# A two-block network on one core: the expert table U split into float16 halves ahead of time and kept in DRAM

## The chip, the core and the metric

The kernel runs on one core of a Trainium2 chip. A core has a matrix engine (TensorE, PE in the profile), three engines that work on rows of 128 partitions (VectorE: DVE, ScalarE: ACT, GpSimd: POOL) and SyncE (SP), which here only issues transfers. Each engine carries out its own instructions strictly in order and waits on semaphores for the others. Sixteen DMA engines move data between DRAM and the on-chip memory; the transfers that one engine issues form a queue. The metric is the device time of one execution in microseconds (us).

## What is computed

Two transformer blocks follow each other for 512 tokens of width 1024, all in float32.

- The first block is a root-mean-square norm, three kinds of attention (a causal one with a forget gate, "fox"; a dilated one; one over compressed, selected and window keys, "NSA"), a gated sum of the three, and a gated feed-forward network with a short convolution.
- The second block is a norm, a mixer (short convolution and a gated linear recurrence) and PEER: a layer of 16384 experts, each a row of U and a row of V.

```python
q = (xt @ wq).reshape(t, PEER_HEADS, 2, HALF_Q)
scores = jnp.einsum('thpd,hpnd->thpn', q, keys)
s_top, i_top = lax.top_k(scores, PEER_TOPK)
cand = s_top[:, :, 0, :, None] + s_top[:, :, 1, None, :]
c_score, c_idx = lax.top_k(cand..., PEER_TOPK)
expert = i1 * N_KEYS + i2
gates = jax.nn.softmax(c_score, axis=-1)
u = jnp.take(u_tab, eb, axis=0)
a = jax.nn.gelu(jnp.einsum('td,thkd->thk', xb, u))
w = gb * a
vv = jnp.take(v_tab, eb, axis=0)
y = jnp.einsum('thk,thkd->td', w, vv)
```

## The kernel before, in words

**Products.** PE multiplies float16, so each float32 operand is split into a high half and a low half that together hold it, and each product is three matmuls (high by high, low by high, high by low). A weight block of 128 x 2048 float32 (1 MB) is loaded by SP into a tile `w` (`w_dma`, L136), ACT writes the high half `whi` (L144) and DVE the low half `wlo` (the helper `stt`, L72). The list `seq` fixes the order of all blocks that go this way; its last 64 blocks are the whole of U, transposed (`u_t`). The function `w_get` returns the next split block and keeps one further block split and one more loaded. Two `w` tiles are kept, and three pairs of halves.

**First block.** The norm and the first projections come first. The dilated attention follows; its three outputs are merged in `dil_merge` (L730 to L756: a maximum, three exponentials, a reciprocal and products, handed to and fro between DVE, POOL and ACT). Then come the fox attention, whose tables are built by PE from a triangular constant (`fox_tables`, L761; the constant `c_tri`, 128 x 1508 float32, loaded once at the start of the program, L462), and the NSA attention. Between the strips of the attention PE is given the remaining projections and gates as filling. The three outputs are multiplied by w_p and w_o, and the feed-forward (`conv_ffn`) follows: 22 blocks of w_up, each evacuated by ACT (`acc`), DVE (`acc`, `u`) and POOL (`ul`), then 12 blocks of w_down.

**Second block.** The mixer, the PEER queries, and the choice of the experts (called routing below): DVE finds the top 16 of many rows (`cand`, `cs`, `ci`), POOL and DVE turn the places into expert numbers (`eq` L1501, `sel` L1503), and PE transposes them (`pq`, L1526). 384 of the tokens are treated densely: all 16384 experts are computed as U times h, blocks of U being multiplied by 384 columns, 48 matmuls a block. A gate matrix G is built (`g`, `pg`), multiplied with the activations, and the result multiplied by V (64 more float32 blocks, split as `vh` and `vl`). The other 128 tokens gather their own rows of U and V: 128 gathers of each, issued by POOL (`row`, L1332). The first 12 blocks of U are multiplied beside the routing, 22 beside the building of G, and the last 30 in turn with blocks of V.

The order of the instructions on each engine is settled when the program is built, by a scheduler that simulates it; the code gives dependences and a rough order.

Of the kernel before, what the change touches and what calls it, by code (L numbers as in the profile page):

```python
# [9 lines left out]
F32 = mybir.dt.float32  # L10
# [8 lines left out]
S = 512  # L19
# [39 lines left out]
def tile_net(ctx: ExitStack, tc: tile.TileContext, xT, pp, cc, tn, btm, w_a, w_misc, cmp_w1, cmp_w2, cmp_pe,  # L59
# [68 lines left out]
    w32s, whs = {}, {}  # L128

    def w_dma():  # L130
        i = wst["dma"]
        if i >= len(seq):
            return
        t = wp.tile([128, 2048], F32, tag="w32", name="w32")
        n = seq[i].shape[1]
        nc.sync.dma_start(out=t[:, :n], in_=seq[i])  # L136
        w32s[i] = t[:, :n]
        wst["dma"] += 1
# [8 lines left out]
    def w_split():  # L147
        i = wst["split"]
        if i >= len(seq):
            return  # L150
        while wst["dma"] <= i:
            w_dma()
        t = w32s.pop(i)
        n = t.shape[1]
        pool = wst["more"] if wst["more"] is not None and i % 3 == 2 else wp
        hi = pool.tile([128, 2048], F16, tag="whi", name="whi")[:, :n]
        lo = pool.tile([128, 2048], F16, tag="wlo", name="wlo")[:, :n]
        split(t, hi, lo, wst["after"].pop(0) if wst["after"] else ())
        whs[i] = (hi, lo)
        wst["split"] += 1  # L160
# [10 lines left out]
    def mm3(ps, wh, wl, ah, al, idx, start=True, stop=True):  # L171

        n = len(idx)
        for j, i in enumerate(idx):
            mm(ps, wh(i), ah(i), start and j == 0, False)
            mm(ps, wh(i), al(i), False, False)
            mm(ps, wl(i), ah(i), False, stop and j == n - 1)

    def ps512(tag="mm", bufs=None):
# [173 lines left out]
    env = locals()  # L353
    attention(tc, nc, env)
    conv_ffn(tc, nc, env)
    mixer(tc, nc, env)
    peer(tc, nc, env)
# [91 lines left out]
def attention_core(tc, nc, env, ctx, yh, yl, gates, gate):  # L449
# [10 lines left out]
    while len(e.w32s) < 2:  # L460
        e.w_dma()
    e.load_consts(qp, nc.sync, "tri", "cmpm")  # L462

# [8 lines left out]
    nc.sync.dma_start(out=pe_t, in_=e.cmp_pe)  # L472


    F = {}
    scale_of = {t: 0.125 * DS if t in (0, 1, 4, 5, 6, 10, 11, 12) else DS for t in range(17)}

    def fm_tile(hi, lo, half, t, ps=None):
# [3 lines left out]
        if t in (13, 14):  # L482


            c = ap.tile([128, 2, 256], F32, tag="cf", name="cf", bufs=1)
            for g in range(2):
                rows = slice(64 * g, 64 * g + 64)
                for par in range(2):
                    SC.activation(out=c[64 * par:64 * par + 64, g, :], in_=ps[rows, par::2], func=ACTF.Identity, scale=DS,
                                  bias=bfm[rows, t:t + 1])  # L490
            for j in range(2):
                a = ap.tile([128, 2, 256], F32, tag="ca", name="ca", bufs=1)
# [3 lines left out]
                ch = qp.tile([128, 2, 256], F16, name=f"ch{t}{j}")  # L496
                cl = qp.tile([128, 2, 256], F16, name=f"cl{t}{j}")
# [338 lines left out]

    ptc = qp.tile([96, 4, 2, 128], F32, name="ptc")

    def cmp_probs(i):
# [25 lines left out]
        for g in range(2):  # L865
            PE.transpose(pt[0:96, g * 128:g * 128 + 128], st[:, 3 * g:3 * g + 3, :].rearrange("p h c -> p (h c)"), ident)
        V.tensor_copy(out=ptc[:, i], in_=pt[0:96, 0:256].rearrange("p (g c) -> p g c", g=2))

    def nsa_strips(r, sp):
# [4 lines left out]
        for i in range(4):  # L874
            n = 128 * (i + 1)
            for br in range(2):
# [3 lines left out]
                    gate=lambda p, i=i, br=br: gsig[:, i, 3 * (3 * p + r) + 1 + br:3 * (3 * p + r) + 2 + br],  # L880
                    extra=(lambda p, i=i: (F["vc"][32 * r:32 * r + 31, p, :], ptc[32 * r:32 * r + 31, i, p, :])) if br == 0 else None,
                    v=lambda b, p, br=br: T["vsw", b][:, br * 128 + p * 64:br * 128 + p * 64 + 64],
# [13 lines left out]
    for t in range(4):  # L896
        fm_tile(None, None, None, 4 + t, outs[t][2])
    e.x0s.close()
    dil = ExitStack()
    dp = dil.enter_context(tc.tile_pool(name="dp", bufs=1))  # L900
# [36 lines left out]
    dil.close()  # L937
    stk.append(ctx.enter_context(tc.tile_pool(name="stk", bufs=1)))
    with tc.tile_pool(name="fox", bufs=1) as sp:
        fox_tables(0, sp)  # L940
        run(fox_strips(0), n1 + (n2 - n1) // 2, NST - 1)
        fox_tables(1, sp)
        run(fox_strips(1), n2, NST - 1)
    with tc.tile_pool(name="nsa", bufs=2) as sp:
        rest = len(fill) - n2
# [875 lines left out]
```

## Time and profile before

| | us |
|---|---|
| median of 3 runs | 2386.96 |
| lowest and highest run | 2384.31, 2392.14 |
| the profiled execution | 2390.82 |
| span of its instructions | 2389.1 |

| engine | busy, share of the span |
|---|---|
| PE | 2278.6 us, 95% |
| DVE | 1682.6 us, 70% |
| ACT | 946.6 us, 40% |
| POOL | 783.1 us, 33% |

The mean granted clock of PE is 0.981 of its full 2.4 GHz. A busy PE is not PE at full rate: where the granted clock is 0.5, a matmul takes twice its time and counts as busy. So two figures are read together for each stretch: the time in which PE did nothing, and the clock.

### The profile page before, as it was taken

What the parts mean: (1) busy time and instruction counts of PE and PEld (TensorE: products, weight loads), DVE (VectorE), ACT (ScalarE), POOL (GpSimd) and SP (SyncE); (2) the same over time, 40 slices, a digit from 0 to 9 for tenths busy, and PEclk for the clock granted to TensorE, in tenths of its full rate; (3) what the DMA queues carried; (4) which work ended last, traced back from release to release, by engine and by line L of the source; (5) the groups of instructions that cost most, each with busy time, mean ns of one, the idle gap of its engine ahead of it and who ended that gap; (6) DMA issues with size and microseconds to landing.
All of it is one profiled execution on the core that took longest, in us unless ns stands there. A gap on an engine that the chain in (4) does not pass through costs nothing.

```text
span 2389.1 us, 35874 instructions
## 1 busy us (share of the span) xinstructions
PE 2278.6 (95%) x14415; PEld 1373.9 (58%) x14415; DVE 1682.6 (70%) x2996; ACT 946.6 (40%) x1256; POOL 783.1 (33%) x518
## 2 busy tenths in 40 slices
PE   7989999999999998999998789999999999989997
PEld 5646655456444466665745456665565555555665
DVE  5575556546444346554799989997898888899787
ACT  4454334334333226233424337775333332232332
POOL 1021000102222002220101541114667776778773
PEclk9998899999999999999999899999999999999998
DMA  5212321232222222211223548999999999899983
GB/s 195 89 36 89 119 69 54 88 106 89 106 106 96 98 90 94 88 54 71 108 87 132 185 151 315 341 328 358 350 345 348 358 342 342 320 370 389 379 304 124
DMA packets 143111, 460.64 MB, mean 193 GB/s; under 512 B 10864, under 2 KB 64496, under 8 KB 114656
## 3 DMA queue, kind: packets, MB, share of 16 engines
q1 hardware_dynamic: 92096, 280.02, 32.7%
q0 software_dynamic: 37600, 138.56, 15.6%
q10 hardware_dynamic: 13248, 39.76, 4.3%
q8 instruction: 113, 1.85, 0.3%
q14 instruction: 54, 0.44, 0.1%
HBM read 417.14 MB, written 40.63 MB: 192 GB/s over the span
## 4 chain that ended last, share of the span: by engine, by line
PE 59%; DVE 19%; issue 8%; DMA 6%; POOL 4%; ACT 3%; ACTq 0%; POOLq 0%; DVEq 0%; SPq 0%
PE mm L67 34%; PE y L67 5%; PE pa L67 5%; PE pb L67 5%; DVE wlo L72 3%; DMA row<-in_v_n,idx 3%; DVE row L1339 2%; DMA row<-in_u_n,idx 2%; PE o L67 2%; PE s L67 2%; PE p L67 2%; POOL row L1332 2%; POOL a L1622 1%; ACT whi L144 1%; PE t L643 1%
## 5 line engine op out<-in xcount | busy, mean ns | idle before, releaser
L67 PEld LDWEIGHTS <-whi 128*128 128x128 f16 x5384 | 530.1, 99 | 431.8 <-issue 42.8
L67 PE MATMUL mm<-hh,whi 128*128 128x384 f16 (+2 forms) x1640 | 566.7, 346 | 23.3 <-DVE x L72 11.9
L67 PE MATMUL mm<-hl,whi 128*128 128x384 f16 (+2 forms) x1640 | 567.3, 346 | 0.0
L67 PE MATMUL mm<-hh,wlo 128*128 128x384 f16 (+2 forms) x1640 | 566.8, 346 | 0.0
L72 DVE SCALAR_TENSOR_TENSOR wlo<-w,whi 128x2048 f16<-128x2048 f32 (+1 forms) x160 | 371.9, 2325 | 163.6 <-ACT whi L144 163.3
L144 ACT ACTIVATE whi<-w 128x2048 f16<-128x2048 f32 (+1 forms) x160 | 303.4, 1898 | 318.9 <-PE mm L67 219.6
L67 PEld LDWEIGHTS <-wlo 128*128 128x128 f16 x2692 | 266.8, 99 | 207.8 <-issue 9.6
L1332 POOL DMA_INDIRECT row<-in_u_n,idx x128 | 204.0, 1594 | 243.4 <-DVE atok L1339 225.7
L67 PEld LDWEIGHTS <-vh 128*128 128x128 f16 x2112 | 206.5, 98 | 131.2 <-issue 2.5
L144 ACT ACTIVATE vh<-w 128x2048 f16<-128x2048 f32 x64 | 119.0, 1903 | 345.0 <-PE mm L67 284.2
L1332 POOL DMA_INDIRECT row<-in_v_n,idx x128 | 211.0, 1649 | 108.9 <-DVE ytok L1356 81.0
L67 PE MATMUL y<-wl,vh 128*128 128x384 f16 (+2 forms) x660 | 212.8, 323 | 6.1 <-DVE wl L1624 5.9
L67 PE MATMUL y<-wh,vl 128*128 128x384 f16 (+2 forms) x660 | 212.8, 323 | 0.0
L67 PE MATMUL y<-wh,vh 128*128 128x384 f16 (+2 forms) x660 | 212.7, 323 | 0.0
L1356 DVE SCALAR_TENSOR_TENSOR ytok<-row,atok,ytok 128x1024 f32<-128x1024 f32 x127 | 184.6, 1453 | 26.6 <-DMA row<-in_v_n,idx 22.9
L1339 DVE CUSTOM_DVE_ANT_0 row<-row,htok 128x1024 f32<-128x1024 f32 x128 | 175.5, 1394 | 22.3 <-DMA row<-in_u_n,idx 22.1
L72 DVE SCALAR_TENSOR_TENSOR vl<-w,vh 128x2048 f16<-128x2048 f32 x64 | 153.5, 2412 | 25.5 <-ACT vh L144 25.4
L1622 POOL TENSOR_TENSOR a<-a,g 128x768 f32<-128x768 f32 x64 | 141.5, 2217 | 27.6 <-DMA g<-gd 18.0
L67 PEld LDWEIGHTS <-vl 128*128 128x128 f16 x1056 | 103.9, 98 | 71.4 <-issue 7.3
L67 PE MATMUL mm<-wh,vh 128*128 128x384 f16 (+2 forms) x396 | 126.6, 321 | 0.9 <-DVE x L72 0.9
L67 PE MATMUL mm<-wl,vh 128*128 128x384 f16 (+2 forms) x396 | 126.6, 321 | 0.0
L67 PE MATMUL mm<-wh,vl 128*128 128x384 f16 (+2 forms) x396 | 126.6, 321 | 0.0
(400 smaller groups left out, 3634.0 us busy)
## 6 DMA issues: line engine op xcount, KB each, us to landing
w<-in_u_t SPq DMA_DIRECT2D x64, 1024.0 KB
w<-in_v_t SPq DMA_DIRECT2D x64, 1024.0 KB
w<-in_w_a SPq DMA_DIRECT2D x24, 1024.0 KB
gd<-stage ACTq DMA_DIRECT2D x48, 512.0 KB
g<-gd SPq DMA_DIRECT2D x32, 768.0 KB
w<-in_w_up SPq DMA_DIRECT2D x22, 1024.0 KB
w<-in_w_mix SPq DMA_DIRECT2D x14, 1024.0 KB
ga<-a ACTq DMA_DIRECT2D x34, 384.0 KB
```

What stands on the lines that cost most here:

```text
L67: i = PE.matmul(out=out, lhsT=lhsT, rhs=rhs, start=start, stop=stop)
L72: (eng or V).scalar_tensor_tensor(out=out, in0=in0, scalar=scalar, in1=in1, op0=op0, op1=op1)
L144: SC.activation(out=hi, in_=t, func=ACTF.Copy, scale=WS)
L643: PE.transpose(ps[:, b * 128:b * 128 + 128], s.e[:, p, b * 128:b * 128 + 128], ident)
L1332: GP.indirect_dma_start(out=row, out_offset=None, in_=tab, in_offset=bass.IndirectOffsetOnAxis(ap=idx[:, s:s + 1], axis=0))
L1339: V.tensor_tensor_reduce(out=row, in0=row, in1=tok[kind[s // 32]], scale=1.0, scalar=0.0, op0=ALU.mult, op1=ALU.add, accum_out=atok[:, s:s ...
L1356: i = V.scalar_tensor_tensor(out=ytok[n], in0=row, scalar=w, in1=ytok[n], op0=ALU.mult, op1=ALU.add)
L1622: GP.tensor_tensor(out=by, in0=by, in1=g[:, :, i, :], op=ALU.mult)
```

## The change

Sixty-four blocks of U are split early. Each is cut in four quarters of 128 x 512. For a quarter POOL issues a load from `u_t` (256 KB, L143 of the changed file), ACT writes the high half and DVE the low half into a tile `ehl` (two of them exist; the loads have three), and POOL issues a store of both halves to a tensor `early` in DRAM (256 KB in 256 rows of 1 KB, L149). A step (`early_step`) stores the quarter split before, splits the next and issues the loads up to two quarters ahead; it is taken each time that PE has been given another 6100 columns of matmuls by `fm`, `tm` or `mm3`, from the dilated attention to the end of the feed-forward. What would be left then is done before the mixer.

In PEER a block of U then comes as two loads of 512 KB from `early`, straight into `whi` and `wlo`, with no work for ACT and DVE (L208, L209).

To make room, the constants `tri` to `cmpm` (the tile `c_tri`) and the tile `ptc` now lie in the pool `stk`, which is opened when the dilated attention's pool is closed, and are loaded there; some small tiles share buffers.

```diff
+NPRE = 64
+PACE = (6100, 6100)
...
+    dr0 = ctx.enter_context(tc.tile_pool(name="dr0", bufs=1, space=DRAM))
+    eps_ = ctx.enter_context(ExitStack())
+    ep = eps_.enter_context(tc.tile_pool(name="ep", bufs=3))
+    early = {len(seq) - 64 + k: dr0.tile([128, 2, 2048], F16, name=f"early{k}") for k in range(NPRE)}
+    es = {"load": 0, "split": 0, "store": 0, "cols": 0, "pace": 0, "t": {}, "h": {}}
+
+    def early_load():
+        q = es["load"]
+        if q < 4 * NPRE:
+            t = es["t"][q] = ep.tile([128, 512], F32, tag="e32", name="e32")
+            GP.dma_start(out=t, in_=u_t[q // 4][:, q % 4 * 512:q % 4 * 512 + 512])
+            es["load"] += 1
+
+    def early_store():
+        q = es["store"]
+        if q < es["split"]:
+            GP.dma_start(out=early[len(seq) - 64 + q // 4][:, :, q % 4 * 512:q % 4 * 512 + 512], in_=es["h"].pop(q))
+            es["store"] += 1
+
+    def early_step():
+
+        early_store()
+        q = es["split"]
+        if q < es["load"]:
+            h = es["h"][q] = ep.tile([128, 2, 512], F16, tag="ehl", name="ehl", bufs=2)
+            split(es["t"].pop(q), h[:, 0], h[:, 1])
+            es["split"] += 1
+        while es["load"] < min(es["split"] + 2, 4 * NPRE):
+            early_load()
...
+    def pace(cols):
+        if es["pace"]:
+            es["cols"] += cols
+            while es["cols"] >= es["pace"]:
+                es["cols"] -= es["pace"]
+                early_step()
...
-        split(t, hi, lo, wst["after"].pop(0) if wst["after"] else ())
+        if t is None:
+            nc.sync.dma_start(out=hi, in_=early[i][:, 0])
+            nc.sync.dma_start(out=lo, in_=early[i][:, 1])
+        else:
+            split(t, hi, lo, wst["after"].pop(0) if wst["after"] else ())
...
             mm(ps, wl(i), ah(i), False, stop and j == n - 1)
+            pace(3 * S)
...
-    e.load_consts(qp, nc.sync, "tri", "cmpm")
...
     dil.close()
     stk.append(ctx.enter_context(tc.tile_pool(name="stk", bufs=1)))
+    e.load_consts(stk[0], nc.sync, "tri", "cmpm")
+    ptc.append(stk[0].tile([96, 4, 2, 128], F32, name="ptc"))
```

Three places of the order are shown, since the diff alone does not tell them. The first is SP, the queue that issues the loads of weights and constants. Before, `c_tri` is the fourth transfer of the program:

```order
L342 DMA x_94<-in_xT 128x4x256 x4
L136 DMA w_238<-in_w_a 128x2048
L136 DMA w_240<-in_w_a 128x2048
L101 DMA c_tri<-in_cc 128x1508
L469 DMA btm<-in_btm 128x918
```

In the changed kernel it stands between the loads of the blocks for the compressed keys (`in_cmp_w`):

```order
L185 DMA w_2038<-in_w_a 128x2048
L185 DMA w_2191<-in_cmp_w 128x2048
L103 DMA c_tri<-in_cc 128x1508
L185 DMA w_2313<-in_cmp_w 128x2048
L185 DMA w_2521<-in_w_a 128x2048
L185 DMA w_2680<-in_cmp_w 128x2048
```

The load has moved from the program's start to the place behind `dil_merge`. In the built program it waits for the last reads of the tiles whose room it takes, among them the subtractions that give `yl` at the end of `dil_merge` (L327 of the changed file, on DVE and POOL).

The second is PE at that place in the changed kernel; the order is the same before. `lsm` is the input of `dil_merge`, `lf` that of the fox tables, and `hh`, `whi` are operands of the filling:

```order
L69 MATMUL mm<-c_ident,lsm 64x128 x10
L69 MATMUL mm<-c_tri,lf 128x512
L69 MATMUL mm<-c_tri,lf 128x384
L69 MATMUL mm<-c_tri,lf 128x256
L69 MATMUL mm<-c_tri,lf 128x128
L69 MATMUL mm<-c_tri,lf 128x512
L69 MATMUL mm<-c_tri,lf 128x384
L69 MATMUL mm<-c_tri,lf 128x256
L69 MATMUL mm<-c_tri,lf 128x128
L69 LDWEIGHTS whi
L69 MATMUL mm<-hh_64,whi 128x512
```

The matmuls that read `c_tri` have not moved: they stand right behind those that start `dil_merge` and ahead of the filling.

The third is DVE in `dil_merge`, as changed:

```order
L803 TENSOR_TENSOR lsx<-ls_1800,ls_1801 128x512
L801 COPY ls_1802<-mm 128x4x128
L74 SCALAR_TENSOR_TENSOR ehl<-e_2384,ehl 128x512
L804 TENSOR_TENSOR lsx<-lsx,ls_1802 128x512
L74 SCALAR_TENSOR_TENSOR ehl<-e_2427,ehl 128x512
L74 SCALAR_TENSOR_TENSOR ehl<-e_2457,ehl 128x512
L812 TENSOR_TENSOR oy_957<-oy_957,ls_1800 128x512
...
L810 RECIPROCAL lsx<-lsx 128x512
L74 SCALAR_TENSOR_TENSOR ehl<-e_2534,ehl 128x512
L74 SCALAR_TENSOR_TENSOR ehl<-e_2552,ehl 128x512
L327 TENSOR_TENSOR yl_272<-oy_957,yh_264 128x512
L327 TENSOR_TENSOR yl_274<-oy_959,yh_266 128x512
```

Low halves of early quarters now stand between the steps of the merge. Over the whole order of DVE there are 256 of them: 37 ahead of the merge's first copy, 6 inside it, 122 from there to the first evacuation of the feed-forward, 61 up to its last, and 30 beside w_down; none is left for the mixer. In PEER the 64 `wlo` of U are gone from DVE and the 64 `whi` from ACT.

## Rows read from the trace of the kernel before

**Rows 1.** The page, part 2: busy tenths of DVE in 40 slices of 59.7 us

```profile
DVE  5575556546444346554799989997898888899787
```

**Rows 2.** Busy time by stretch, columns named in its first line

```profile
core 0: us, PE busy (x) PEld busy (x) DVE busy (x) ACT busy (x) POOL busy (x), PEclk, DMA share, GB/s
...
60.00:250.00 190.00, 180.18 (x1269) 116.50 (x1268) 106.91 (x312) 90.74 (x189) 21.33 (x14) 0.91 0.21 73
250.00:500.00 250.00, 248.21 (x1333) 128.05 (x1332) 135.37 (x373) 90.30 (x176) 9.87 (x10) 0.99 0.23 83
500.00:800.00 300.00, 298.46 (x1584) 154.82 (x1583) 138.08 (x155) 112.82 (x132) 65.58 (x32) 1.00 0.28 100
...
1260.00:1425.00 165.00, 139.69 (x833) 82.15 (x832) 152.73 (x518) 59.48 (x67) 68.24 (x81) 0.95 0.45 160
1425.00:1650.00 225.00, 222.56 (x1858) 150.57 (x1857) 203.65 (x268) 158.39 (x172) 41.05 (x26) 1.00 0.90 328
1650.00:2100.00 450.00, 430.70 (x2621) 257.31 (x2619) 394.32 (x388) 145.39 (x135) 317.68 (x188) 0.99 0.93 343
...
2350.00:2389.00 39.00, 24.01 (x233) 22.04 (x232) 24.51 (x56) 10.63 (x26) 4.67 (x7) 0.82 0.22 68
```

**Rows 3.** Groups of instructions, 1260 to 1425 us (columns as in part 5)

```profile
L1501 POOL TENSOR_TENSOR eq<-eq,sif 128x256 f16<-128x256 f16 x64 | 53.5, 871 | 53.6 <-DVE eq L1497 49.8 <-DVE cs L1419 3.8
L72 DVE SCALAR_TENSOR_TENSOR wlo<-w,whi 128x2048 f16<-128x2048 f32 x17 | 40.1, 2359 | 0.0
L144 ACT ACTIVATE whi<-w 128x2048 f16<-128x2048 f32 x16 | 30.5, 1908 | 36.6 <-PE mm L67 25.1 <-DMA w<-in_u_t 11.5
...
L1503 DVE TENSOR_REDUCE sel<-eq 128x128 f32<-128x2048 f16 x8 | 18.2, 2275 | 11.3 <-POOL eq L1501 11.3
```

**Rows 4.** Waits of PE, 1260 to 1425 us: total, times, longest

```profile
PE pq L1526 <- DVE sel L1503: 16.9, 5, 10.4
```

**Rows 5.** Waits of PE, 1425 us to the end

```profile
PE mm L67 <- DVE x L72: 12.8, 8, 3.9
```

**Rows 6.** DMA of 1700 to 1900 us: queues and issues

```profile
q0 software_dynamic: 10114, 36.83, 48.5%
...
row<-in_u_n,idx POOLq DMA_INDIRECT x73
```

**Rows 7.** Timeline of PE, 134 to 163 us: start, length, engine, line, operation

```profile
137.71 6.27 PE L67 MATMUL mm<-c_tri,lf 128*128 128x512 f32 x16 [2.80 <-DVE ls L741]
...
156.14 0.38 PE L67 MATMUL mm<-hh,wlo 128*128 128x512 f16 x1
161.21 1.43 PE L67 MATMUL s<-f,f 64*128 64x256 f32 x4 [4.69 <-DVE m L621]
```

**Rows 8.** Timeline of DVE, 134 to 163 us

```profile
156.63 1.70 DVE L494 TENSOR_TENSOR ca<-cf,pe_t 128x256 f32<-128x256 f32 x2
159.03 0.69 DVE L499 TENSOR_TENSOR cl<-ca,ch 128x512 f16<-128x512 f32 x1 [0.70 <-ACT ch L498]
159.64 0.69 DVE L272 TENSOR_TENSOR yl<-oy,yh 128x512 f16<-128x512 f32 x1
```

**Rows 9.** Transfers of 0 to 60 us, a number for each slice of 1.5 us

```profile
GB/s 0 54 316 387 341 359 393 431 410 417 412 327 126 273 344 0 0 0 5 180 426 382 350 71 0 0 0 57 289 14 0 0 87 382 300 371 257 5 0 0
```

**Rows 10.** Timeline of SP, 36 to 48 us

```profile
40.40 0.33 SPq L101 DMA_DIRECT2D c_g<-in_cc  x1
```

**Rows 11.** Busy time by stretch, ahead of the merge (columns as in rows 2)

```profile
60.00:137.00 77.00, 74.60 (x650) 49.68 (x648) 41.40 (x174) 38.35 (x95) 0.00 (x0) 1.00 0.24 83
```

**Rows 12.** Instructions and issues of POOL: the two table loads of the attention

```profile
L871 POOL DMA_DIRECT2D tn<-in_tn x2: 544/576/607, 253.1 to 253.7; - x2
```

**Rows 13.** Transfers of 1270 to 1274 us, a number for each slice of 0.1 us

```profile
GB/s 0 0 0 0 0 0 0 0 0 0 0 0 0 0 0 0 0 0 0 0 338 399 430 399 307 461 430 399 399 307 62 0 0 0 0 0 0 0 0 0
```

**Rows 14.** Timeline of ACT, 1270 to 1276 us

```profile
1271.17 0.34 ACTq L1399 DMA_DIRECT2D ga<-a  x1
```

**Rows 15.** DMA queue that carries the weights, 500 to 800 us

```profile
q1 hardware_dynamic: 4175, 29.88, 28.1%
```

More of the change, by code (lines that the diff above doesn't have):

```diff
@@ L128, in tile_net, with early_end @@
     w32s, whs = {}, {}
+    dr0 = ctx.enter_context(tc.tile_pool(name="dr0", bufs=1, space=DRAM))
[23 more added lines that the diff above has]
+            early_load()
+    def early_end():
+        while es["split"] < 4 * NPRE:
+            early_step()
+        early_store()
+        eps_.close()
+    def pace(cols):
[3 more added lines that the diff above has]
+                es["cols"] -= es["pace"]
+                early_step()
     def w_dma():
@@ L132, in w_dma @@
         if i >= len(seq):
+            return
+        if i in early:
+            wst["dma"] += 1
             return
@@ L152, in w_split @@
             w_dma()
-        t = w32s.pop(i)
-        n = t.shape[1]
+        t = w32s.pop(i, None)
+        n = 2048 if t is None else t.shape[1]
         pool = wst["more"] if wst["more"] is not None and i % 3 == 2 else wp
@@ L195, in tm @@
             mm(ps, hl[k][:, tsl], h3[:, k, c0:c0 + w], False, k == KT - 1)
+            pace(3 * w)
     scratch = {}
@@ L354, in tile_net @@
     attention(tc, nc, env)
+    es["pace"] = PACE[1]
     conv_ffn(tc, nc, env)
+    es["pace"] = 0
+    early_end()
     mixer(tc, nc, env)
@@ L472, in attention_core @@
     nc.sync.dma_start(out=pe_t, in_=e.cmp_pe)
+    cps = []
     F = {}
@@ L482, in fm_tile @@
         if t in (13, 14):
-            c = ap.tile([128, 2, 256], F32, tag="cf", name="cf", bufs=1)
+            c = ap.tile([128, 2, S], F32, tag="pt", name="cf", bufs=2)[:, :, 0:256]
             for g in range(2):
@@ L491, in fm_tile @@
             for j in range(2):
-                a = ap.tile([128, 2, 256], F32, tag="ca", name="ca", bufs=1)
+                a = ap.tile([128, 2, S], F32, tag="e", name="ca", bufs=3)[:, :, 0:256]
                 for g in range(2):
@@ L495, in fm_tile @@
                                     in1=pe_t[:, None, 8 * j:8 * j + 8].to_broadcast([128, 32, 8]), op=ALU.add)
-                ch = qp.tile([128, 2, 256], F16, name=f"ch{t}{j}")
-                cl = qp.tile([128, 2, 256], F16, name=f"cl{t}{j}")
+                ch = cps[0].tile([128, 2, 256], F16, name=f"ch{t}{j}")
+                cl = cps[0].tile([128, 2, 256], F16, name=f"cl{t}{j}")
                 SC.activation(out=ch, in_=a, func=ACTF.Copy)
@@ L834, in compress @@
                               in_=ps[32 * r:32 * r + 31, 0:128].rearrange("p (g d) -> p g d", g=2))
-    ptc = qp.tile([96, 4, 2, 128], F32, name="ptc")
+    ptc = []
     def cmp_probs(i):
@@ L866, in cmp_probs @@
             PE.transpose(pt[0:96, g * 128:g * 128 + 128], st[:, 3 * g:3 * g + 3, :].rearrange("p h c -> p (h c)"), ident)
-        V.tensor_copy(out=ptc[:, i], in_=pt[0:96, 0:256].rearrange("p (g c) -> p g c", g=2))
+        V.tensor_copy(out=ptc[0][:, i], in_=pt[0:96, 0:256].rearrange("p (g c) -> p g c", g=2))
     def nsa_strips(r, sp):
@@ L880, in nsa_strips @@
                     gate=lambda p, i=i, br=br: gsig[:, i, 3 * (3 * p + r) + 1 + br:3 * (3 * p + r) + 2 + br],
-                    extra=(lambda p, i=i: (F["vc"][32 * r:32 * r + 31, p, :], ptc[32 * r:32 * r + 31, i, p, :])) if br == 0 else None,
+                    extra=(lambda p, i=i: (F["vc"][32 * r:32 * r + 31, p, :], ptc[0][32 * r:32 * r + 31, i, p, :])) if br == 0 else None,
                     v=lambda b, p, br=br: T["vsw", b][:, br * 128 + p * 64:br * 128 + p * 64 + 64],
@@ L898, in attention_core @@
     e.x0s.close()
+    cmps = ExitStack()
+    cps.append(cmps.enter_context(tc.tile_pool(name="cps", bufs=1, side="right")))
+    e.es["pace"] = PACE[0]
     dil = ExitStack()
@@ L943, in attention_core @@
         run(fox_strips(1), n2, NST - 1)
+    cmps.close()
     with tc.tile_pool(name="nsa", bufs=2) as sp:
```

## The prediction

> **What bounds the kernel now.** I read the busy time by stretch first [rows 2]. What PE loses in a stretch is its idle time plus the part of its busy time that a lowered clock adds, (1 - clock) x busy. From 1260 to 1425 us, the routing, that is 165 - 139.69 = 25.3 and 0.05 x 139.69 = 7.0, together 32.3 us. While G is built (1425 to 1650) it is 2.4 us, in the alternation of U and V (1650 to 2100) 19.3 + 4.3 = 23.6 us, in the tail (from 2350) 19.3 us. Ahead of that, 60 to 250 us lose 9.8 + 16.2 = 26 us, 250 to 500 us 4.3 us, and the feed-forward (500 to 800) 1.5 us. So PE is the bound almost everywhere, and only a stretch with losses has something to give. The slices of DVE [rows 1] show where that could be: eight tenths or more from slice 23 on, four to five through the first block. In the routing DVE is busy 152.73 of 165 us [rows 2], and 17 low halves of U take 40.1 us of it [rows 3]; PE waits there for `sel`, 16.9 us in all [rows 4]. After 1425 us PE's largest wait is for DVE's `x`, 12.8 us [rows 5]; DVE is busy 394 of 450 us there. In this second place the DMA engines are nearly full too: a share of 0.90 to 0.93 against 0.23 to 0.28 in the first block [rows 2].
>
> **What the change takes away.** In PEER, 64 low halves of 2.36 us on DVE and 64 high halves of 1.91 us on ACT [rows 3]: 151 and 122 us.
>
> Routing: without the 40.1 us, DVE has 112.6 us to do in 165, and PE's 139.69 us are 132.7 at full clock. PE becomes the bound, and at most the 32.3 us are won. At least: the chain from POOL's `eq` (64 x 0.87 = 53.5 us, for which `sel` waits 11.3 us on DVE [rows 3]) stays, and with it PE's 16.9 us and the clock's 7.0; that leaves 8 us. I take 24, nearer the upper end, since a DVE that is 93% busy is the nearest row to full and drops to 68%.
>
> Building of G: 2.4 us at most, taken as 2. U and V in turn: at most 23.6 us, at least nothing, if the transfers become the bound. The bytes do not shrink (two halves of 512 KB for one block of 1 MB), and at a share of 0.93 they have 31 of 450 us to spare. I take 14, about the waits for `x` [rows 5], which hang on DVE's queue. The tail stays: it belongs to the gathers of V.
>
> Sum of the gains: 24 + 2 + 14 = 40 us, between 8 and 58.
>
> **What it adds.** 256 steps. On DVE a low half of 128 x 512 costs about the 0.69 us of `yl` [rows 8], 177 us in all; on ACT no more. On POOL a load and a store cost up to 0.61 us each [rows 12].
>
> Before the merge: 37 steps, some 30 of them from 60 to 137 us. There PE is busy 74.6 of 77 us, DVE 41.4, ACT 38.4 [rows 11]. 30 x 0.69 = 21 us more bring DVE to 62 of 77 and ACT to about 59. In a softmax that passes from PE to DVE to ACT and back, some waits appear: I take 6 us, between 0 and 20 (a 0.69 us halt at each step).
>
> The merge: `c_tri` now waits for the end of it. Before, PE did the fox tables at 137.71 us and the filling up to 156.52, beside the merge [rows 7]. Now both wait, since PE's order has not moved. The last `yl` ends at 159.64 + 0.69 = 160.3 us [rows 8]. The load follows: 512 KB were issued at 40.40 [rows 10], and their last bytes moved just after 43.5 [rows 9], 3.2 us; 754 KB need 0.6 more at the rates of that row, so 3.8 us. PE starts at 164.2, has the same 18.8 us to do, and reaches `s<-f` at 183.0 instead of 161.2 [rows 7]: 21.8 us later. `ca` and `cl`, 2.4 us ahead of the last `yl` on DVE [rows 8], come from the filling and so will come behind it: 19.4. The six quarters inside the merge, 6 x 0.69 = 4.1 us, partly stand where DVE waits for POOL. I take 19, with 15 and 28 as ends (28: each pair of quarters waits some 3 us for a store's landing, and DVE with it).
>
> After the merge: 122 steps up to the feed-forward, 61 up to its last evacuation, one per 3.2 us or so. DVE goes from about 50% to 70% and ACT from 38% to under 60%, PE has little to lose in the row of before, and the cover is that weights are split a whole block ahead (10.24 us of matmuls). A step's half megabyte costs the DMA engines, at 28.1% x 16 x 300 us for 29.88 MB [rows 15], 45 us per MB, that is 1.5 us of the sixteen; beside a share of 0.28 that makes 0.75. I take 2 us up to 500 and 3 us in the feed-forward, between 0 and 40 together. Nothing is left for the mixer.
>
> POOL issues all these transfers in one queue. Before, that queue took 73 gathers in 200 us, 36.83 MB [rows 6]: 0.18 MB per us, at a share of 0.485; a step needs 0.52 MB per 3.2 us, 0.16. So the queue has carried such a rate.
>
> The Trainium skill (DMA: Bandwidth & Descriptors, sections Measured and Anatomy of one DMA) wants batches of 1 MiB or more, and puts a transfer from POOL at some 2.0 us fixed plus its bytes over 436 GB/s; were these paid one after the other, an estimate from that page is 5.2 us for a step's two transfers, which speaks against quarters. A rule of that kind, priced from rows, is a rival below.
>
> Sum: 6 + 19 + 2 + 3 = 30 us. Net -40 + 30 = -10 us. The profiled execution, 2390.8 us, lies 3.9 above the median of 2387.0; against that median the forecast is **2377 us**, by itself 2369 to 2387.
>
> **The rivals.** *All of the relief arrives.* Routing, G and the alternation give 58 us, the early work costs only the wait for `c_tri` and a few us: -58 + 22 = -36, 2351 us. For it: DVE is the fullest engine next to PE in all the stretches that lose. Against it: POOL's `eq`, and the share of 0.93.
>
> *The quarters pace the first block* (slower). There are two tiles `ehl`; the third quarter's high half on ACT, and all that is queued behind it there (exponentials, weight halves), waits until the first one's store has landed. A store: issue 0.61 [rows 12], then the landing. 384 KB issued at 1271.17 [rows 14] had moved at 1273.1 on idle engines [rows 13], 1.9 us. With twice 0.69 for ACT and DVE that is 3.9 us for two steps, and 6100 columns at 2.4 GHz are 2.54 us, 5.1 for two: enough. It decides when a landing takes over 3.1 us. Beside a weight block it may: its packets take 1349 / 4175 = 0.323 us [rows 15], eight per DMA engine, 2.6 us in all, so a landing of 4.5 and 3.25 us a step; at 4.9, 3.45. At 3.35 the 30 early steps lose 0.81 each and the 183 later ones 0.15: 51 us in place of 11. -40 + 19 + 51 = +30, **2417 us** (2396 to 2439).
>
> *The relief is swallowed.* In the alternation the transfers bind (share near 1.0) and the routing hangs on POOL's `eq`: -8 - 2 instead of -40, the costs stay: +20, 2407 us. For it: 0.93 already, and a block's load can now begin only when a pair of halves is free, without two float32 blocks ahead of it. Against it: 15 us pass there for each pair of blocks, and routing has a share of 0.45.
>
> *Transfers are paid by count.* If each transfer of POOL's queue, whatever its size, took the 200 / 73 = 2.74 us of a gather [rows 6], a step would need 5.5 us: (5.5 - 2.54) x 30 + (5.5 - 3.2) x 183 = 510 us, some 2870. Against it: those 2.74 us hold 512 KB at a share of 0.485, so the row gives no sign of a price apart from the bytes.
>
> *It does little.* Were waits before and after equally covered, 2387.
>
> **How the numbers follow.** A difference below 0.3% (7.2 us, 2379.8 to 2394.1) is about what cannot be told from none. Chances: forecast 0.40 (of it 0.25 faster, 0.15 same), full relief 0.22, quarters pace 0.20, relief swallowed 0.14, by count 0.02, little 0.02. Faster 0.25 + 0.22 = 0.47, same 0.17, slower 0.36. The range reaches from the full relief with the early costs at their low ends (-58 + 15, and the 4 us that the tail's clock adds: 2340) to 2430, inside the second rival; about one in eight lies above it, and one in twenty below.
>
> **What would show it.** Right: PE idle from about 138 to 164 us with the tables waiting for the transfer of `c_tri`; everything from 180 us on some 20 to 27 us later; the routing about 24 us shorter, with DVE near 70% and `sel` still waiting for POOL; the alternation some 14 us shorter at a DMA share of 0.95 or more. Wrong: waits of ACT for the landing of `early` through the first block and PE idle in the feed-forward (second rival); PE waiting for the loads of `whi` after 1650 us at a share near 1 (third); a gap at the merge under 10 us.

## The result, and the profile after

The changed kernel takes 2465.0 us (median of 4 runs, 2461.2 to 2476.3) against 2386.6 us before: ratio 1.0328, 95% interval 1.0308 to 1.0349. It is 78 us slower; 2377 was forecast, 2340 to 2430 the range. The lines of the page that answer to those of before: the busy time, the chain that ended last, and two of the groups of transfers with the KB of each and the us from issue to landing.

```profile
PE 2301.7 (93%) x14415; PEld 1382.7 (56%) x14415; DVE 1716.6 (70%) x3188; ACT 973.2 (39%) x1448; POOL 1044.6 (42%) x1030
...
PE 55%; DMA 17%; DVE 14%; issue 7%; ACT 4%; POOL 3%; ACTq 0%; DVEq 0%; POOLq 0%; SPq 0%
PE mm L69 36%; DMA early<-ehl 14%; PE y L69 10%; DVE ehl L74 3%; PE pg L69 2%; ACT whi L193 2%; PE o L69 1%; PE s L69 1%; ACT ehl L193 1%; DVE wlo L74 1%; DVE ytok L1420 1%; DMA row<-in_v_n,idx 1%; DVE mr L1482 1%; PE kv L69 1%; PE t L701 1%
...
e<-in_u_t POOLq DMA_DIRECT2D x256, 256.0 KB, 5.1
early<-ehl POOLq DMA_DIRECT2D x256, 256.0 KB, 4.3
```

DVE's and ACT's busy time are about as before; the low and high halves of U have moved, and cost a little more in quarters. What is new stands in the chain: 14% of the span, some 345 us, are waits for the landing of `early`. A store of a quarter lands 4.3 us after its issue in the median; the spread over all 256 (tile `ehl`, from the start of the issue to the landing) is

```profile
DMA to landing us min/median/max: 2.5/4.3/9.1
```

ACT's waits in the first 1000 us show what waits for it (total, times, longest):

```profile
ACT ehl L193 <- DMA early<-ehl: 294.9, 150, 6.3
ACT acc L1041 <- DVE acc L74: 48.6, 20, 2.9
```

and those of PE, in the same stretch:

```profile
PE mm L69 <- DMA c_tri<-in_cc: 29.5, 1, 29.5
PE mm L69 <- DVE x L74: 23.6, 7, 7.4
PE pa L69 <- DVE acc L74: 13.4, 11, 1.9
```

The busy time by stretch (columns as in rows 2), at the merge, the feed-forward up to its last evacuation, from there to the mixer, the routing, and the alternation with the tail up to the last product with V:

```profile
158.00:188.00 30.00, 0.52 (x7) 0.30 (x4) 19.25 (x19) 9.32 (x15) 18.98 (x22) 0.55 0.52 154
...
640.00:884.00 244.00, 227.26 (x1057) 102.24 (x1055) 148.12 (x149) 115.02 (x149) 118.86 (x148) 1.00 0.70 221
884.00:1021.00 137.00, 115.43 (x677) 67.81 (x676) 68.65 (x87) 57.00 (x78) 41.30 (x64) 0.93 0.62 203
...
1378.00:1519.00 141.00, 123.06 (x738) 73.14 (x736) 116.38 (x487) 27.12 (x46) 52.36 (x81) 0.94 0.54 170
...
1742.00:2448.00 706.00, 702.73 (x4401) 427.41 (x4401) 588.14 (x543) 193.44 (x197) 492.91 (x290) 1.00 0.93 348
```

The stages of before that answer to the routing and the alternation are these rows of the trace before:

```profile
1264.00:1431.00 167.00, 141.89 (x847) 83.50 (x846) 154.73 (x516) 60.37 (x68) 68.24 (x81) 0.95 0.46 162
...
1653.00:2373.00 720.00, 695.52 (x4315) 422.42 (x4314) 630.64 (x560) 229.80 (x212) 507.76 (x289) 0.99 0.91 335
```

At the merge PE is busy 0.52 of 30 us: a gap as it was forecast, 20 us later. The feed-forward, where before lost next to nothing, takes 240 us from its first evacuation to its last, where it took 207. Of these 33 us PE is idle some 17 (244 - 227.26 in the row); in most of the rest it does 67 matmuls with w_down, which before all came behind the last evacuation. From there to the mixer it loses 21.6 + 8.1 us more, idle and clock. PE's losses in the second block (idle plus clock, as in the prediction) fall from 25.1 + 7.1 = 32.2 to 17.9 + 7.4 = 25.3 us in the routing, and from 24.5 + 7.0 = 31.4 to 3.3 us in the alternation. So the second block wins about what was forecast, and the first block loses far more.

Where the time goes is best read from markers, the start or end of one instruction that both traces have. The first line gives before's time in us, the others how much later (+) each kernel reaches the same point; the kernels below the first two are the experiments.

| | first matmul of the fox tables | first product with w_p | first evacuation (`acc`) | last evacuation | first `kv` of the mixer | first `pq` | last `pq` | last `y` |
|---|---|---|---|---|---|---|---|---|
| before | 137.7 | 421.0 | 569.6 | 776.6 | 903.6 | 1180.7 | 1424.5 | 2372.8 |
| the change | +50.1 | +48.0 | +73.8 | +107.2 | +118.0 | +118.4 | +87.6 | +75.5 |
| tri_only | +32.1 | +22.5 | +22.5 | +22.5 | +23.1 | +22.2 | +23.9 | +16.3 |
| tri_early | +19.9 | +24.7 | +56.1 | +89.8 | +113.0 | +113.3 | +82.4 | +73.8 |
| half | +45.0 | +40.0 | +40.0 | +40.0 | +40.0 | +40.1 | +8.2 | +15.5 |
| f34_e2 | +6.9 | +4.3 | +22.4 | +54.9 | +81.7 | +86.5 | +55.9 | +69.9 |
| f34_e6 | +7.9 | +6.4 | +26.6 | +42.7 | +36.6 | +33.8 | +3.4 | +12.2 |
| f12_e4 | +7.1 | +2.2 | +21.1 | +21.7 | +21.7 | +21.7 | -3.7 | +13.7 |
| first12 | +0.1 | +0.8 | +0.8 | +7.7 | +7.7 | +7.7 | -17.5 | -1.2 |
| first30 | -0.1 | +0.3 | +0.3 | +7.6 | +5.1 | +4.2 | -26.2 | -17.5 |
| late30 | +0.2 | -0.6 | -0.6 | +6.6 | +1.8 | -0.2 | -0.3 | -29.3 |
| late30_e3 | 0.0 | -0.1 | -0.1 | +33.1 | +49.5 | +47.8 | +47.7 | +19.7 |
| late30_e2 | 0.0 | -1.0 | -1.0 | +27.0 | +55.2 | +87.7 | +87.7 | +58.0 |
| late40 | +0.2 | -1.0 | -1.0 | -0.2 | +8.2 | +17.2 | +17.1 | -10.0 |

The change is 118 us late at the mixer and wins 43 of them back in PEER. A caution for the last column: tri_only splits nothing early, and its PEER still came out 6 us shorter than before's in the one profiled execution, so differences of some 8 us behind the mixer are not read as effects from one trace. And in the kernels with steps in the feed-forward some of w_down is multiplied ahead of the last evacuation, so that column is not all loss; the next one is.

### The profile page after: what moved, and what is told of

Read it like the earlier page. It is cut to its first block, busy times and chain, and to the rows that moved or that the text cites. A ratio compares the mean times of both kernels' runs of the same rounds, so it can differ in the third digit from the quotient of the medians.

```text
span 2465.7 us, 37621 instructions
## 1 busy us (share of the span) xinstructions
PE 2301.7 (93%) x14415; PEld 1382.7 (56%) x14415; DVE 1716.6 (70%) x3188; ACT 973.2 (39%) x1448; POOL 1044.6 (42%) x1030
## 3 DMA queue, kind: packets, MB, share of 16 engines
q0 software_dynamic: 78560, 272.81, 32.2%
## 4 chain that ended last, share of the span: by engine, by line
PE 55%; DMA 17%; DVE 14%; issue 7%; ACT 4%; POOL 3%; ACTq 0%; DVEq 0%; POOLq 0%; SPq 0%
PE mm L69 36%; DMA early<-ehl 14%; PE y L69 10%; DVE ehl L74 3%; PE pg L69 2%; ACT whi L193 2%; PE o L69 1%; PE s L69 1%; ACT ehl L193 1%; DVE wlo L74 1%; DVE ytok L1420 1%; DMA row<-in_v_n,idx 1%; DVE mr L1482 1%; PE kv L69 1%; PE t L701 1%
## 5 line engine op out<-in xcount | busy, mean ns | idle before, releaser
L149 POOL DMA_DIRECT2D early<-ehl x256 | 180.9, 706 | 515.6 <-DVE ehl L74 379.4
L74 DVE SCALAR_TENSOR_TENSOR ehl<-e,ehl 128x512 f16<-128x512 f32 x256 | 195.4, 770 | 244.4 <-ACT ehl L193 244.1
L1396 POOL DMA_INDIRECT row<-in_u_n,idx x128 | 179.9, 1405 | 264.7 <-DVE atok L1403 227.9
L193 ACT ACTIVATE ehl<-e 128x512 f16<-128x512 f32 x256 | 160.0, 625 | 307.8 <-DMA early<-ehl 294.9
L74 DVE SCALAR_TENSOR_TENSOR wlo<-w,whi 128x2048 f16<-128x2048 f32 (+1 forms) x96 | 219.6, 2287 | 75.8 <-ACT whi L193 75.4
L1403 DVE CUSTOM_DVE_ANT_0 row<-row,htok 128x1024 f32<-128x1024 f32 x128 | 171.6, 1358 | 49.5 <-DMA row<-in_u_n,idx 49.3
L193 ACT ACTIVATE whi<-w 128x2048 f16<-128x2048 f32 (+1 forms) x96 | 180.4, 1881 | 47.7 <-PE mm L69 45.2
L143 POOL DMA_DIRECT2D e<-in_u_t x256 | 172.2, 673 | 1.7 <-issue 1.6
L1444 ACT ACTIVATE a<-mm 128x384 f32<-128x384 f32 x128 | 62.3, 491 | 267.2 <-PE mm L69 251.5
```

Of the source, the lines that this page charges most:

```text
L74: (eng or V).scalar_tensor_tensor(out=out, in0=in0, scalar=scalar, in1=in1, op0=op0, op1=op1)
L143: GP.dma_start(out=t, in_=u_t[q // 4][:, q % 4 * 512:q % 4 * 512 + 512])
L149: GP.dma_start(out=early[len(seq) - 64 + q // 4][:, :, q % 4 * 512:q % 4 * 512 + 512], in_=es["h"].pop(q))
L193: SC.activation(out=hi, in_=t, func=ACTF.Copy, scale=WS)
L1396: GP.indirect_dma_start(out=row, out_offset=None, in_=tab, in_offset=bass.IndirectOffsetOnAxis(ap=idx[:, s:s + 1], axis=0))
L1403: V.tensor_tensor_reduce(out=row, in0=row, in1=tok[kind[s // 32]], scale=1.0, scalar=0.0, op0=ALU.mult, op1=ALU.add, accum_out=atok[:, s:s ...
```

## The experiments

Times are medians; each ratio is to runs of the kernel before on the same chip. Two theories are set against each other: C, that a step waits for a free tile `ehl`, that is for the landing of a store; and W, that a step costs by the work that it puts on ACT, DVE and the transfers.

**The late constant by itself, and taken away.** tri_only keeps the moved constant and tiles and splits nothing early; tri_early is the change with the constant loaded at the start.

```diff
tri_only
-NPRE = 64
+NPRE = 0
tri_early
     while len(e.w32s) < 2:
         e.w_dma()
+    e.load_consts(qp, nc.sync, "tri", "cmpm")
...
-    e.load_consts(stk[0], nc.sync, "tri", "cmpm")
```

> The change with no block of U split early (NPRE 0): what remains is that c_tri is loaded behind the merge of the dilated attention, and the moved tiles. If the late load alone costs what its place suggests: c_tri lands near 164 us, PE idle some 25 us at the merge, some 19 us lost there and up to 9 of them won back in the strips that follow: 2397 to 2408. If the wait is harmful only because the quarters stretch the merge: within 5 us of before.

> The change with c_tri loaded at the program's start as before, all else kept (64 blocks, 6100 columns, two tiles ehl). If the wait of 29.5 us for c_tri is a loss of its own: 20 to 30 us faster than the change, 2435 to 2445, and the rest of the early loss (some 90 us) stays. If the landing of the stores fills the same time anyway: within 8 us of the change.

tri_only: 2408.7 us, ratio 1.0081 (1.0055 to 1.0106), 19.5 us slower than before. tri_early: 2458.2 us, 1.0291 (1.0270 to 1.0313), only 7 us faster than the change. The first is near what the prediction said of this term (19 us), though not all of it is the load: f34_e2, f34_e6 and f12_e4 below have the moved tiles too, but the constant at the start and no step before the feed-forward, and they are 6.9 to 7.9 us late at the fox tables and 2.2 to 6.4 at w_p. So of the 22.5 us at w_p in tri_only some 16 to 20 are the load's. PE's one long wait in tri_only, 60 to 300 us:

```profile
PE mm L69 <- DMA c_tri<-in_cc: 22.6, 1, 22.6
```

In the second the other branch held, within 8 us of the change: with the constant on time the kernel is 23 us earlier at w_p (+24.7 against +48.0) and then loses all but 5 of them again before the mixer. ACT's waits in tri_early, the same stretch as above, have not changed:

```profile
ACT ehl L193 <- DMA early<-ehl: 298.4, 155, 8.1
```

The 256 low halves on DVE span 11.5 to 983 us in the change and 10.5 to 992 us in tri_early: 3.8 us a step in both. I read this so: what ends the first block is not the sum of its stalls but the row of steps, and a stall elsewhere, as that at the merge, mostly runs beside it. It rests on this one pair.

**Half as many steps at half the pace.**

```diff
-NPRE = 64
-PACE = (6100, 6100)
+NPRE = 32
+PACE = (12200, 12200)
```

> The change with 32 blocks and one step per 12200 columns (5.1 us) in place of 64 and 6100; c_tri still late, two tiles ehl. Theory C: 5.1 us is more than the 3.7 us that two tiles need, so what is left of the early loss is the wait for c_tri and a little, 25 to 40 us, against some 30 us won in the routing: 2380 to 2400. Theory W: 21 + 128 x 0.38 = 70 us lost: 2425 to 2435.

2420.4 us, 1.0131 (1.0103 to 1.0160). It lies between the two ranges and did not tell the theories apart, because the pace did not hold: the 128 steps were all done by 505 us, again one per 3.9 us, with ACT waiting 107 us for landings. The order of the instructions is settled by simulation, and the steps, which nothing ties to their place, came earlier than the pace asked. What it does show: once the steps are over, at 505 us, nothing more is lost (+40.0 from w_p to the mixer), 18 us beyond tri_only.

**The number of tiles `ehl`, first pair.** 34 blocks, steps only from the feed-forward on, the constant early; two tiles against six (and three against four for the loads).

```diff
-NPRE = 64
-PACE = (6100, 6100)
+NPRE = 34
+PACE = (0, 6100)
...
     attention(tc, nc, env)
+    epl.append(eps_.enter_context(tc.tile_pool(name="ep", bufs=4)))
     es["pace"] = PACE[1]
...
-            h = es["h"][q] = ep.tile([128, 2, 512], F16, tag="ehl", name="ehl", bufs=2)
+            h = es["h"][q] = epl[0].tile([128, 2, 512], F16, tag="ehl", name="ehl", bufs=6)
```

> 34 blocks (136 steps) split early, the steps only from the start of the feed-forward on, two tiles ehl as in the change, c_tri loaded at the start as before. Theory C (the wait for the landing of a store, 4.3 us median, before one of the two tiles is free: some 3.7 us a step at best, with ACT, DVE and then PE held behind it): 136 steps x (3.7 - 2.5) us of pace = some 45 to 60 us lost in the feed-forward, against some 31 us won in the routing and little more: 2395 to 2415. Theory W (each step costs by the work it puts on ACT, DVE and the transfers, (118 - 21) / 256 = 0.38 us): 136 x 0.38 = 52 us lost, also 2395 to 2415. The pair with six tiles tells them apart.

> The same 34 blocks in the feed-forward, with six tiles ehl and four for the loads in place of two and three. Theory C: the landing is hidden, at most 15 us are lost in the feed-forward: 2360 to 2375, at least 25 us faster than with two tiles, and ACT's wait for the landing of early nearly gone. Theory W: as with two tiles, 2395 to 2415.

f34_e2: 2456.8 us, 1.0271 (1.0246 to 1.0296). f34_e6: 2409.7 us, 1.0080 (1.0057 to 1.0104). They are 42 and 35 us above the upper ends that theory C gave, and the second, taken by itself, lies in the range of theory W. But their difference, 47 us, is of C's size, where W had none, and with two tiles ACT waits 194 us for landings, with six 4 us. What is left with six tiles has another cause, at least in part: ACT now waits for loads (510 to 950 us),

```profile
ACT ehl L193 <- DMA e<-in_u_t: 74.6, 67, 4.0
```

and the markers show 20 us lost between w_p and the first evacuation, where the norm stands. So free tiles alone do not make the steps cost nothing.

**Where the steps stand.** f12_e4 is the same construction with 12 blocks, a step per 12200 columns and four tiles. first12 starts from the kernel before, so all moved tiles are back in place, and puts three steps behind the `ul` of each block of w_up, queued on POOL after it. It also has six tiles and six for the loads, issued up to four quarters ahead.

```diff
f12_e4
+NPRE = 12
+PACE = (0, 12200)
first12
+    KS = list(range(12))
...
-            e.hilo(u, uh[j], ul[j], 1)
+            SC.activation(out=uh[j], in_=u, func=ACTF.Copy)
+            lo = GP.tensor_tensor(out=ul[j], in0=u, in1=uh[j], op=ALU.subtract)
+            with tc.issue_after(lo.ins):
+                for _ in range(3):
+                    e.early_step()
```

> Only the 12 blocks that the routing multiplies (48 steps), one step per 12200 columns from the feed-forward on, four tiles ehl, c_tri loaded at the start. Theory C: nothing lost in the feed-forward, the routing's 26 to 31 us won: 2355 to 2362, faster than before. Theory W: 48 x 0.38 = 18 us lost: 2374 to 2379. If the relief of the routing depended on the rest of U too: 2387.

> The first 12 blocks only (48 steps), three steps behind each block of w_up, none in the norm's lead. The kernel with 12 blocks that began at the feed-forward's start lost 19 us up to the first evacuations, 15 of them in the lead. If that was the quarters in the lead: the feed-forward loses at most 6 us here, and some 8 us are won behind it: 2380 to 2388, at least 12 us faster than that kernel. If it was their number: again 15 us or more lost, 2395 to 2403.

f12_e4: 2403.2 us, 1.0055 (1.0033 to 1.0077); 2355 to 2362 was expected. first12: 2387.9 us, 0.9994 (0.9984 to 1.0003), 15 us faster, as its first branch had it. The markers show both halves of the first kernel's miss. First, f12_e4 goes from +2.2 to +21.1 us between w_p and the first evacuation, where the norm and the lead of the feed-forward stand; first12 has no step there and loses nothing (+0.8). ACT in that place of f12_e4 (timeline, as rows 14):

```profile
574.10 0.63 ACT L193 ACTIVATE ehl<-e 128x512 f16<-128x512 f32 x1 [3.88 <-DMA e<-in_u_t]
575.34 0.63 ACT L193 ACTIVATE ehl<-e 128x512 f16<-128x512 f32 x1 [0.61 <-DMA e<-in_u_t]
575.88 0.81 ACT L326 ACTIVATE hh<-h 128x256 f16<-128x256 f32 x2
```

A quarter whose load has not landed stands on ACT ahead of `hh`, the operand that PE waits for. How much of the 15 us is the place of the steps, and how much the loads that are issued further ahead, is not separated. Second, the routing's gain is not one: first12 has `pq` done 25 us earlier relative to the routing's start (+7.7 to -17.5), and all but 9 us are gone at the end, no more than the caution above allows. A routing that ends sooner has multiplied fewer blocks of U (the change's routing holds 738 matmuls, that of before 847, by their rows), and PE does them in the stages behind it, where the change loses next to nothing.

**Which blocks.** The same construction with six tiles, six for the loads, four steps behind each `ul`, and 30 blocks: the first or the last.

```diff
first30
+    KS = list(range(30))
late30
+    KS = list(range(34, 64))
```

> Built on the kernel before: only the last 30 blocks of U, those that alternate with V, are split early (120 steps), all in the feed-forward, each group of four steps queued on POOL behind the ul of a block of w_up, so that none falls into the norm's lead; six tiles ehl, six for the loads; c_tri as before. Theory A (the loss of the alternation, 24 to 31 us, is DVE's and goes when its low halves go; the routing keeps its own): the alternation wins 20 to 28 us, the routing nothing, the feed-forward loses 10 to 20: 2375 to 2392. Theory R (the routing's relief is what the change wins, and the alternation's goes only with it): at most 8 us won, 2390 to 2405.

> The same with the first 30 blocks of U, those beside the routing and the building of G. Theory A: the routing wins some 7 us, the building of G 2, the alternation nothing; the feed-forward loses as in the kernel with the last 30: 2388 to 2400, 8 to 20 us slower than that one. Theory R: 20 us or more won: 2375 to 2385, faster than that one.

late30: 2368.8 us, 0.9923 (0.9898 to 0.9949), faster than before. first30: 2377.4 us, 0.9956 (0.9944 to 0.9968). Theory A had the sign and the order right; both were better than it said, since 120 steps cost nothing in late30 (markers: -0.2 at the first `pq`). The 2377 of first30 lies in the range of theory R, which, however, had it faster than late30, and it is 9 us slower. In late30 PE's losses are, by stretch (feed-forward, routing, alternation; columns as in rows 2):

```profile
569.00:905.00 336.00, 332.76 (x1721) 168.32 (x1719) 234.88 (x263) 186.47 (x254) 199.71 (x266) 1.00 0.83 287
1264.00:1424.00 160.00, 136.71 (x803) 79.68 (x802) 147.74 (x504) 57.41 (x64) 68.19 (x81) 0.94 0.45 161
...
1637.00:2344.00 707.00, 703.66 (x4411) 428.20 (x4409) 589.94 (x544) 192.83 (x197) 493.71 (x290) 1.00 0.93 348
```

The feed-forward loses 3.2 us and the routing keeps its 23.3 + 8.2 = 31.5; the alternation loses 3.3 instead of 31.4. So the alternation's loss goes with the splits of its own 30 blocks. That it was DVE's part of them and not ACT's is argued from the row of before (DVE busy 631 of 720 us, ACT 230) and from PE's waits for `x` [rows 5]. That first30 wins too, theory A did not say: it is 22 us shorter from the first `pq` to the end. I did not separate what of this comes from the building of G and what from the gathers of U, which start 12 us earlier there.

**The number of tiles, second pair, and a third value.** late30 with two and with three tiles; nothing else is changed.

```diff
-            h = es["h"][q] = epl[0].tile([128, 2, 512], F16, tag="ehl", name="ehl", bufs=6)
+            h = es["h"][q] = epl[0].tile([128, 2, 512], F16, tag="ehl", name="ehl", bufs=2)
```

> The kernel with the last 30 blocks (120 steps, free of cost in the feed-forward with six tiles ehl) with two tiles as in the change, nothing else changed. Theory C (the landing of the store before last holds ACT): 3.6 to 3.8 us a step as in the change, 120 steps = 430 to 450 us where the feed-forward behind the lead has 320: 40 to 80 us slower than with six tiles, 2410 to 2450, and ACT waiting 100 us or more for the landing of early. If the tiles did not matter and the change lost by where its steps stand (attention, lead): within 10 us of 2369.

> As the last two with 30 blocks, three tiles ehl. Theory C, by the time that a tile is bound (two steps of 3.7 us, 7.4 us): three tiles give one step per 2.5 us, 120 steps = 296 us, inside the feed-forward's 320: 2369 to 2385, nearly all of the 85 us between two and six tiles back. If the landing grows as the steps come faster: between, 2395 to 2430.

late30_e2: 2454.0 us, 1.0279 (1.0260 to 1.0299), 85 us slower than with six tiles and 64 us slower than before, 4 us above theory C's range. ACT waits 95 us for landings, just under the 100 that were expected. late30_e3: 2412.0 us, 1.0084 (1.0057 to 1.0112). Theory C holds for two tiles; for three the plain division of 7.4 us by three was too kind, as its other branch said. The trace gives, from the view of the tile `ehl` (its first row, ACT's instructions with the first and the last start, and its last), for two tiles

```profile
L191 ACT ACTIVATE ehl<-e x120: 612/629/632, 582.0 to 1013.6; 128x512 f16<-128x512 f32 x120
...
DMA to landing us min/median/max: 2.5/4.8/8.2
```

for three

```profile
L191 ACT ACTIVATE ehl<-e x120: 612/629/632, 582.6 to 927.7; 128x512 f16<-128x512 f32 x120
...
DMA to landing us min/median/max: 2.5/5.6/9.7
```

and for six

```profile
L191 ACT ACTIVATE ehl<-e x120: 612/614/631, 582.7 to 861.9; 128x512 f16<-128x512 f32 x120
...
DMA to landing us min/median/max: 3.0/6.5/12.1
```

One step per 3.63, 2.90 and 2.35 us (the span of starts over 119), and the landing's median grows with the rate, 4.8, 5.6 and 6.5 us, presumably because more stores and loads are under way at once. Not all of the 85 us is lost in the feed-forward: with two tiles the steps last until 1014 us and run into the mixer, which begins at 959; the markers show 55 us up to there and 33 more up to the first `pq`, most of it one wait of PE (959 to 1268 us) for an instruction that DVE has behind the last steps:

```profile
PE mm L67 <- DVE qq L72: 29.9, 2, 27.5
```

How a landing of 5 us stops PE is seen on ACT and DVE. ACT in the change, from 690 us on:

```profile
691.55 0.63 ACT L193 ACTIVATE ehl<-e 128x512 f16<-128x512 f32 x1 [2.45 <-DMA early<-ehl]
692.09 1.89 ACT L193 ACTIVATE whi<-w 128x2048 f16<-128x2048 f32 x1
...
703.72 0.63 ACT L193 ACTIVATE ehl<-e 128x512 f16<-128x512 f32 x1 [3.08 <-DMA early<-ehl]
704.25 1.89 ACT L193 ACTIVATE whi<-w 128x2048 f16<-128x2048 f32 x1
```

and the same place in late30 with six tiles:

```profile
653.11 0.61 ACT L191 ACTIVATE ehl<-e 128x512 f16<-128x512 f32 x1
654.39 1.91 ACT L191 ACTIVATE whi<-w 128x2048 f16<-128x2048 f32 x1 [0.67 <-PE pb L67]
...
663.46 0.61 ACT L191 ACTIVATE ehl<-e 128x512 f16<-128x512 f32 x1
664.75 1.91 ACT L191 ACTIVATE whi<-w 128x2048 f16<-128x2048 f32 x1 [0.67 <-PE pb L67]
```

In the change `whi`, the weights of a coming block, stands directly behind a quarter that waits 3.08 us for a landing, and the two `whi` shown are 704.25 - 692.09 = 12.2 us apart. With six tiles the quarters find a tile free, `whi` waits for PE alone, and the period is 664.75 - 654.39 = 10.4 us, PE's own. But it is not the weights that PE lacks in the change. DVE's order at the same place is

```profile
704.38 0.69 DVE L74 SCALAR_TENSOR_TENSOR ehl<-e,ehl 128x512 f16<-128x512 f32 x1 [4.46 <-ACT ehl L193]
704.99 0.68 DVE L74 SCALAR_TENSOR_TENSOR u<-pb,acc 128x512 f32<-128x512 f32 x1
```

and PE's waits from 640 to 884 us are

```profile
PE pa L69 <- DVE acc L74: 13.4, 11, 1.9
PE pb L69 <- DVE u L74: 2.9, 4, 1.2
PE mm L69 <- DVE wlo L74: 0.5, 1, 0.5
```

The low half waits for the high half, the high half for the landing, and the evacuations `acc` and `u`, which empty the tiles that PE writes next, stand on DVE behind the low half: 16.3 of PE's 16.8 us of waits are for them.

**More steps.**

```diff
-    KS = list(range(34, 64))
+    KS = list(range(24, 64))
...
-                for _ in range(4):
+                for _ in range(5):
```

> The last 40 blocks, five steps behind each block of w_up, six tiles. 160 steps in some 320 us are one per 2.0 us, 1.5 us of all sixteen DMA engines each, beside a share of 0.28: near full. If the transfers still keep up: another 5 us won, 2362 to 2368. If they bind: the feed-forward loses 10 to 30 us, 2372 to 2395.

2385.3 us, 0.9978 (0.9967 to 0.9989): the second branch. The markers show nothing lost up to the last evacuation, 8 us at the mixer and 17 at the first `pq`, with a DMA share over the feed-forward (569 to 912 us) of

```profile
569.00:912.00 343.00, 331.96 (x1690) 165.60 (x1689) 248.50 (x288) 200.23 (x279) 226.99 (x319) 0.98 0.92 321
```

against 0.83 in late30. So the room in the feed-forward ends between 120 and 160 steps. That the transfers bind is not shown by this: the landing's median is 6.5 us as in late30, but the last steps, which end at 862 us in late30, stand at 937 us, inside the mixer, and what they hold up there was not separated from the transfers.

## Why the prediction was wrong

**The step that failed** is the second rival's own arithmetic, by which the forecast left it at 0.20: "3.9 us for two steps, and 6100 columns at 2.4 GHz are 2.54 us, 5.1 for two: enough." The landing in it, 1.9 us, was the last byte of 384 KB on idle engines [rows 13, 14]. The shortest of 256 stores took 2.5 us to land and the median 4.3. With 4.3 the same arithmetic gives (0.61 + 1.38 + 4.3) / 2 = 3.15 us a step, and 3.5 with the median of 5.0 in the feed-forward, both over the 2.54 that were allowed; measured was one step per 3.8 us, and the steps no longer fitted into the first block at the pace of PE. (What is left up to 3.8 is not broken down here.) The forecast had 6 + 2 + 3 = 11 us for all steps; tri_early, with the constant on time, is 113 us late at the mixer. The text had the deciding point right (a landing over 3.1 us); for the forecast it took an idle engine for a row of a stage with a share of 0.28, to which the change itself adds another 0.4 (in the change the queue of the quarters has a share of 0.43 and that of the weights 0.27 from 640 to 884 us; columns as in rows 15, below them the stores of that stretch):

```profile
q0 software_dynamic: 9884, 32.36, 43.0%
q1 hardware_dynamic: 2967, 21.42, 26.6%
...
early<-ehl POOLq DMA_DIRECT2D x63, 256.0 KB, 5.0
```

That the wait is for a free tile, and not the work on ACT, DVE and the transfers, is shown by two against six tiles: 85 us, with the same work in both. The rival that came true was itself too mild: it priced a landing of 4.5 to 4.9 us at 3.25 to 3.45 us a step and gave 2417 us, 2439 at most, against 2465. The change with six tiles was not run; f34_e6 speaks against it being free of loss.

**The attention, 6 us forecast**, was 20 us by the first table matmul in tri_early, where the constant is early. Some 7 of them come with the moved tiles, as the three kernels without a step there show; the other 13 come with the steps, and ACT waits 45.5 us for landings up to 165 us. **The stages after the merge, 2 + 3 us**, were 26 us from w_p to the first evacuation and 44 us from there to the mixer. The forecast counted busy shares (DVE 70%); what counted was one instruction that waited at the head of an engine's order.

**The constant, 19 us**, was right for what it was priced as: 19.5 us by itself, a few of them the moved tiles'. In the change PE waits 29.5 us there: the whole merge comes 20 us later, and the load, issued at 181.6 us, held PE until 187.8, 6.2 us instead of 3.8. Yet its part in the result is no more than what lies between tri_early and the change, 7 us by the medians and 9 by the ratios: the row of steps ends within 9 us of the same time with it or without it. The forecast added terms that do not add.

**The gains, 40 us**, were 43 (from +118.4 to +75.5), in other places than said. The routing gave 7 of the 24, as little as the lower end named there (8), though not with the same parts: PE's waits for `sel`, which that end kept at 16.9 us, fell to one of 9.9, and the clock's part stayed (7.4). PE's waits in the change, 1378 to 1519 us:

```profile
PE pq L1590 <- DVE sel L1567: 9.9, 1, 9.9
```

The 31 us by which the last `pq` comes nearer to before in the markers are mostly matmuls that moved into the stages behind. The alternation gave 28, more than the whole 23.6 that the text saw in its shorter stretch; the transfers did not bind at a share of 0.93. The two misses cancelled: that the sum came out is luck. With 1 us from the building of G these are 36 of the 43; the rest is within the caution above. (Of DVE's slices from the 23rd on, said to be eight tenths or more, three stand at seven; nothing in the sum hangs on it.)

**The transfers paid by count** fell as it was argued: six tiles took a step per 2.35 us, two transfers of 256 KB each, under the 5.5 us of that rival. The rule of the Trainium skill beside it (DMA: Bandwidth & Descriptors, Anatomy of one DMA), 2.0 us plus the bytes over 436 GB/s, gives an estimate of 2.6 us for one store; the fastest one here took 2.5 and the median 4.3, so the trace agrees with it for the fastest stores alone. With that estimate in place of 1.9 the arithmetic would have read 4.6 us for two steps, still under 5.1: what the landing grew by beside the other transfers, which neither figure holds, decided.

## What to carry to other kernels

Work that is moved beside other work must not wait at the head of an engine that feeds or empties the bound one: give its output tiles enough copies to cover the landing of a store under load, not on idle engines, and count the copies times the step against the landing. Before adding up stalls, look for a row of steps with its own length; while it is the longer one, removing a stall beside it wins little (here 5 of 23 us). And move only the work whose relief the trace shows as lost time of the bound engine: here the last 30 of 64 blocks, split in the stage that has room and with six tiles, made the kernel 0.8% faster than before, where all 64 made it 3.3% slower.

## What was not expected of the hardware

The landing of a 256 KB store grew from 4.8 to 6.5 us (medians) as the rate of steps grew from one per 3.63 to one per 2.35 us, although the transfers kept up with the faster steps: a longer landing was no sign here that the queue was full. And a store or load issued from POOL held POOL 0.67 to 0.71 us on average, against 0.54 to 0.61 for the table loads [rows 12]: 180.9 us for the 256 stores of the change and 172.2 for its loads.
